# A column sum of 32768 x 2048 float32: from casting loads with TensorE sums to float32 loads with a running vector sum

## The chip, the core and the metric

The kernel runs on one core of one Trainium2 chip. The metric is the device time of one execution in microseconds. Before the change three runs gave a median of 629.03 us (628.92 to 629.57).

A core has five engines with queues of their own: TensorE (PE, matrix multiply, with PEld for its weight loads), VectorE (DVE), ScalarE (ACT), GpSimd (POOL) and SyncE (SP). DMA transfers are issued from the queue of an engine (here POOL or SP), and 16 DMA engines carry them out. SBUF is the memory on the core with 128 partitions, PSUM is where TensorE writes its sums, and DRAM holds the input and the output.

## The reference

```python
def setup_inputs():
    batch, seq, dim = 32, 1024, 2048
    return {"grad_output": np.random.randn(batch, seq, dim).astype(np.float32)}

def reference(grad_output):
    return np.sum(grad_output, axis=(0, 1)).astype(np.float32)
```

The input is 268.44 MB. Seen as 32768 rows of 2048 float32, it is 256 row blocks of 128 rows. The output is one row of 2048 float32. All the work is one pass over the input.

## The kernel before

The list `plan` (L60 to L85) cuts the 256 row blocks into loads, in this order: two float32 tiles of one row block each, issued from SP; 30 tiles of eight row blocks and one of two, then a taper of four and two, all issued from POOL; five tiles of one row block; and the last row block in four pieces of 512 columns, from the right column group to the left one. All loads from POOL have float16 tiles as their destination, so the DMA casts on the way. A tile of m row blocks gives each partition m neighbouring rows of DRAM, which is one contiguous piece of m x 8 KB.

One loop (L132) goes over the plan. It issues the load (L146). For a float16 tile of more than one row block it adds the tile's two halves on VectorE into `C` (L152, float16). Then it sums over the 128 partitions on TensorE (L161): a matmul with a column of ones as weights and 512 columns of `C` or of the tile as moving data adds one row of 512 sums to one of four PSUM accumulators, one for each group of 512 columns. An eight-row-block tile needs 16 such matmuls after the add. Behind the loop the four accumulators are copied to `res`, by ScalarE (L175) and VectorE (L177) in turn, and one DMA from SP writes the output (L178).

What sets the order: the Tile framework traces the instructions, puts them on the queues of their engines and adds the semaphore waits. Each queue is worked off in order. The pool "io" has three buffers for the large tiles, of 32 KB in each partition, so the load of tile i+3 on POOL waits until L152 has read tile i. The tail tiles have a pool of eight buffers of their own. The SP queue holds the two first loads and the output; POOL's queue holds the other 42 loads. The two float32 tiles are multiplied in float32 with `ones32`, the others in float16 with `ones16`.

```python
nc.vector.tensor_tensor(
    out=C[:], in0=T[:, :half], in1=T[:, half:], op=mybir.AluOpType.add
)
...
nc.tensor.matmul(
    accs[b][:, :],
    lhsT=w[:],
    rhs=red[:, j * MM_N : (j + 1) * MM_N],
```

Of the kernel before, what the change touches and what calls it, by code (L numbers as in the profile page):

```python
# [1 line left out]

# [4 lines left out]

P = 128
MM_N = 512  # L10

PRE_TILES = 2
PRE_M = 1
PRE_ENGS = ("sync", "sync")
BULK_M = 8
BULK_TAPER = (4, 2)
USE_DVE = True
TAIL_TILES = 5
COL_SPLIT_LAST = True
T_BUFS = 3  # L20
C_BUFS = 3
TAIL_BUFS = 8
BULK_ENGS = ("gpsimd",)
OUT_COPY_ENGS = ("scalar", "vector")


@with_exitstack
def kernel(
    ctx: ExitStack,
    tc: tile.TileContext,  # L30
    grad_output: bass.AP,
    out: bass.AP,
):
    nc = tc.nc
    fp32 = mybir.dt.float32
    fp16 = mybir.dt.float16

    D = out.shape[-1]
    flat = grad_output.rearrange("b s d -> (b s) d")
    R = flat.shape[0]  # L40
    assert R % P == 0 and D % MM_N == 0
    nbanks = D // MM_N
    n_row_blocks = R // P

    pre_tiles = min(PRE_TILES, n_row_blocks // PRE_M // 4)
    col_split = COL_SPLIT_LAST and nbanks > 1
    taper = [m for m in BULK_TAPER if m < BULK_M]
    n_small = TAIL_TILES + (1 if col_split else 0)
    while pre_tiles * PRE_M + sum(taper) + n_small > n_row_blocks:
        if TAIL_TILES and n_small > 1:  # L50
            n_small -= 1
        elif taper:
            taper = taper[1:]
        else:
            col_split = False
            n_small = min(n_small, 1)
            break
    n_tail = n_small - (1 if col_split else 0)

    plan: list = []  # L60
    row = 0
    for i in range(pre_tiles):
        plan.append((row, PRE_M, fp32, PRE_ENGS[i % len(PRE_ENGS)], 0, D))
        row += P * PRE_M
    tail_start = R - P * (n_small + sum(taper))
    bi = 0
    while row < tail_start:
        take = min(P * BULK_M, tail_start - row)
        plan.append((row, take // P, fp16, BULK_ENGS[bi % len(BULK_ENGS)], 0, D))
        bi += 1  # L70
        row += take
    for m in taper:
        plan.append((row, m, fp16, BULK_ENGS[bi % len(BULK_ENGS)], 0, D))
        bi += 1
        row += P * m
    for _ in range(n_tail):
        plan.append((row, 1, fp16, BULK_ENGS[bi % len(BULK_ENGS)], 0, D))
        bi += 1
        row += P
    if col_split:  # L80
        for b in range(nbanks - 1, -1, -1):
            plan.append((row, 1, fp16, BULK_ENGS[bi % len(BULK_ENGS)], b * MM_N, MM_N))
            bi += 1
        row += P
    assert row == R  # L85

    io_pool = ctx.enter_context(tc.tile_pool(name="io", bufs=T_BUFS))
    pre_pool = None
    if pre_tiles:
        pre_pool = ctx.enter_context(tc.tile_pool(name="pre", bufs=pre_tiles))  # L90
    c_pool = None
    if USE_DVE:
        c_pool = ctx.enter_context(tc.tile_pool(name="csum", bufs=C_BUFS))
    n_small_tiles = n_tail + (nbanks if col_split else 0)
    tail_pool = None
    if n_small_tiles:
        tail_pool = ctx.enter_context(
            tc.tile_pool(name="tail", bufs=min(n_small_tiles, TAIL_BUFS))
        )
    const_pool = ctx.enter_context(tc.tile_pool(name="const", bufs=1))  # L100
    psum_pool = ctx.enter_context(tc.tile_pool(name="psum", bufs=1, space=bass.MemoryType.PSUM))

    ones16 = const_pool.tile([P, 1], fp16)
    nc.vector.memset(ones16[:], 1.0)  # L104
    ones32 = None
    if pre_tiles:
        ones32 = const_pool.tile([P, 1], fp32)
        nc.vector.memset(ones32[:], 1.0)  # L108

    accs = [  # L110
        psum_pool.tile([1, MM_N], fp32, tag=f"psum{b}", name=f"psum{b}")
        for b in range(nbanks)
    ]
    res = const_pool.tile([1, D], fp32)

    def uses_dve(entry) -> bool:
        _, m, dt_, _, _, col_n = entry
        return USE_DVE and dt_ is fp16 and m > 1 and col_n == D

    def n_chunks(entry) -> int:  # L120
        _, m, dt_, _, _, col_n = entry
        n = (m * col_n) // MM_N
        return n // 2 if uses_dve(entry) else n

    total_mm = [0] * nbanks
    for e in plan:
        for j in range(n_chunks(e)):
            total_mm[((e[4] + j * MM_N) % D) // MM_N] += 1
    started = [False] * nbanks
    n_mm = [0] * nbanks  # L130

    for i, entry in enumerate(plan):  # L132
        row0, m, dt_, eng_name, col_lo, col_n = entry
        rows = flat[row0 : row0 + m * P]
        if col_n == D:
            src = rows.rearrange("(p m) d -> p (m d)", p=P)
        else:
            src = rows[:, col_lo : col_lo + col_n]

        if dt_ is fp16:  # L140
            big = m > 1 and col_n == D
            pool, tag = (io_pool, "T") if big else (tail_pool, "Ttail")
            T = pool.tile([P, m * col_n], fp16, tag=tag, name=f"t{i}")
        else:
            T = pre_pool.tile([P, m * col_n], fp32, tag="Tpre", name=f"t{i}")
        getattr(nc, eng_name).dma_start(out=T[:], in_=src)  # L146

        red = T
        if uses_dve(entry):
            half = (m * col_n) // 2  # L150
            C = c_pool.tile([P, half], fp16, tag="C", name=f"c{i}")
            nc.vector.tensor_tensor(  # L152
                out=C[:], in0=T[:, :half], in1=T[:, half:], op=mybir.AluOpType.add
            )
            red = C

        w = ones16 if dt_ is fp16 else ones32
        for j in range(n_chunks(entry)):
            b = ((col_lo + j * MM_N) % D) // MM_N
            n_mm[b] += 1  # L160
            nc.tensor.matmul(  # L161
                accs[b][:, :],
                lhsT=w[:],
                rhs=red[:, j * MM_N : (j + 1) * MM_N],
                start=(not started[b]),
                stop=(n_mm[b] == total_mm[b]),
            )
            started[b] = True

    bank_order = list(range(nbanks - 1, -1, -1)) if col_split else list(range(nbanks))  # L170
    for k, b in enumerate(bank_order):
        eng = OUT_COPY_ENGS[k % len(OUT_COPY_ENGS)]
        dst = res[:, b * MM_N : (b + 1) * MM_N]
        if eng == "scalar":
            nc.scalar.copy(out=dst, in_=accs[b][:, :])  # L175
        else:
            nc.vector.tensor_copy(out=dst, in_=accs[b][:, :])  # L177
    nc.sync.dma_start(out=out[None, :], in_=res[:])  # L178


# [1 line left out]
_INS = ['grad_output']  # L182
_OUTS = [((2048,), 'float32')]


# [23 lines left out]
```

## Time and profile before

| what | value |
|---|---|
| median of three runs | 629.03 us |
| span of the profiled execution, first to last instruction | 627.2 us |
| busy: PE, DVE, POOL | 195.1, 138.9, 22.6 us |
| L152, adds over 8192 float16 | 30 times, 4.425 us each |
| L161, matmuls on c, 512 columns, float16 | 496 records, 0.533 us on average |
| L146 from POOL, issue | 42 times, 0.538 us each |
| L146 from POOL, 8 row blocks: issue to landing | 53.1 us (median) |
| mean granted TensorE clock | 0.650 |
| DRAM read | 268.44 MB, 428 GB/s over the span |

The page of the profile shows one profiled execution. Its own time is the span of 627.2 us, which begins at the first and ends at the last instruction; a time of a run holds what lies around it as well, and the median of the runs is 1.8 us longer than this span. Rows of groups give the line, the engine, the operation, the tiles, the shapes and the mean length of one instruction; what stands behind the bar is the idle time before them and what ended it. In answers about stretches of time each row gives the busy time of each engine, the granted TensorE clock (1.00 is full), the busy share of the DMA engines and the GB/s that they wrote. A packet is one contiguous piece that one DMA engine moves. In those rows a packet counts where it starts, so a short stretch can show a share over 1 and the next one nearly 0.

### The profile page before, as it was taken

How to read it: one execution, taken by the hardware profiler on the slowest of the kernel's cores; microseconds unless marked ns; L12 is line 12 of the kernel's file. 1: busy time of each engine (PE TensorE's matmuls, PEld its weight loads, DVE VectorE, ACT ScalarE, POOL GpSimd, SP SyncE). 2: the span in 40 equal slices, each digit the busy share in tenths (PEclk: the TensorE clock that was granted, in tenths of full speed). 3: DMA queues.
4: the chain of work that ended last, by engine and by line, in shares of the span. 5: the costliest groups of instructions: out<-in, count | busy, mean ns of one | idle time of the engine just before them, and what ended most of it. 6: DMA issues, size and time to landing. Idle time of an engine off the chain costs nothing.

```text
span 627.2 us, 1267 instructions
## 1 busy us (share of the span) xinstructions
PE 195.1 (31%) x536; PEld 58.1 (9%) x536; DVE 138.9 (22%) x37; ACT 2.4 (0%) x3; POOL 22.6 (4%) x46
## 2 busy tenths in 40 slices
PE   3323320333203333123341134321333312343165
PEld 0001100011000111001110011100111000111011
DVE  0202222022220122211222202222022221122320
ACT  0000000000000000000000000000000000000000
POOL 1000000000000000000000000000000000000110
PEclk9677556775567665667655776656676567665677
DMA  9999999999999999999999999999999999999997
GB/s 242 226 234 201 234 201 234 202 232 203 232 203 232 203 232 203 232 204 230 205 230 205 230 205 230 205 230 206 228 207 228 207 224 211 224 211 221 206 206 139
DMA packets 6344, 135.36 MB, mean 216 GB/s; under 512 B 705, under 2 KB 1217, under 8 KB 1857
## 3 DMA queue, kind: packets, MB, share of 16 engines
q0 software_dynamic: 6048, 133.17, 98.9%
q1 hardware_dynamic: 290, 2.11, 0.9%
q8 instruction: 4, 0.07, 0.0%
q14 instruction: 2, 0.02, 0.0%
HBM read 268.44 MB, written 0.01 MB: 428 GB/s over the span
## 4 chain that ended last, share of the span: by engine, by line
another core or an unknown queue 66%; DVE 21%; DMA 11%; PE 1%; POOL 1%; issue 0%; DVEq 0%; POOLq 0%
DVE c L152 20%; DMA t<-in_grad_output_dram 11%; PE psum L161 1%; POOL t L146 1%; DVEq L152 0%; DVE res L177 0%; POOLq L193 0%
## 5 line engine op out<-in xcount | busy, mean ns | idle before, releaser
L161 PE MATMUL psum<-c,ones 128*1 128x512 f16 x496 | 175.9, 533 | 405.5 <-DVE c L152 405.5
L152 DVE TENSOR_TENSOR c<-t 128x8192 f16<-128x8192 f16 (+2 forms) x33 | 137.5, 4167 | 471.1 <-DMA t<-in_grad_output_dram 471.1
L161 PEld LDWEIGHTS <-ones 128*1 128x1 f16 x520 | 56.5, 109 | 537.5 <-issue 516.4
L146 POOL DMA_DIRECT2D t<-in_grad_output_dram x42 | 22.4, 538 | 590.4 <-DVE c L152 575.3
L161 PE MATMUL psum<-t,ones 128*1 128x512 f16 (+1 forms) x40 | 19.4, 639 | 23.5 <-DMA t<-in_grad_output_dram 23.5
L177 DVE COPY res<-psum 1x512 f32<-1x512 f32 x2 | 1.4, 679 | 13.9 <-PE psum L161 13.9
L161 PEld LDWEIGHTS psum<-t,ones 128*1 128x1 f32 x16 | 1.6, 106 | 27.5 <-DMA t<-in_grad_output_dram 14.1
L175 ACT COPY res<-psum 1x512 f32<-1x512 f32 x2 | 1.1, 575 | 621.1 <-PE psum L161 621.1
L175 ACT ACT_TABLE_LOAD x1 | 1.3, 1283 | 0.7 <-PEq L193 0.7
L104 DVE MEMSET ones<- 128x1 f16 x1 | 0.1, 59 | 0.8 <-PEq L193 0.8
L193 POOL MEMSET const-float32-0.0<- 128x1 f32 x1 | 0.1, 100 | 0.2 <-issue 0.2
L193 POOL MEMSET const-bfloat16-1.0<- 128x1 bf16 x1 | 0.1, 103 | 0.0
L193 POOL MEMSET const-float32-1.0<- 128x1 f32 x1 | 0.1, 100 | 0.0
L193 POOL MEMSET const-uint8-127<- 128x1 uint8 x1 | 0.1, 100 | 0.0
L108 DVE MEMSET ones<- 128x1 f32 x1 | 0.1, 59 | 0.0
## 6 DMA issues: line engine op xcount, KB each, us to landing
t<-in_grad_output_dram POOLq DMA_DIRECT2D x30, 4096.0 KB, 53.1
t<-in_grad_output_dram POOLq DMA_DIRECT2D x5, 512.0 KB, 20.4
t<-in_grad_output_dram SPq DMA_DIRECT2D x2, 1024.0 KB, 14.3
t<-in_grad_output_dram POOLq DMA_DIRECT2D x2, 1024.0 KB, 26.6
t<-in_grad_output_dram POOLq DMA_DIRECT2D x1, 2048.0 KB, 29.0
t<-in_grad_output_dram POOLq DMA_DIRECT2D x4, 128.0 KB, 16.1
out_dram<-res SPq DMA_DIRECT2D x1, 8.0 KB
```

The lines of the kernel that those rows point to most:

```text
L104: nc.vector.memset(ones16[:], 1.0)
L108: nc.vector.memset(ones32[:], 1.0)
L146: getattr(nc, eng_name).dma_start(out=T[:], in_=src)
L152: nc.vector.tensor_tensor(out=C[:], in0=T[:, :half], in1=T[:, half:], op=mybir.AluOpType.add)
L161: nc.tensor.matmul(accs[b][:, :], lhsT=w[:], rhs=red[:, j * MM_N : (j + 1) * MM_N], start=(not started[b]), stop=(n_mm[b] == total_mm[b]),)
L175: nc.scalar.copy(out=dst, in_=accs[b][:, :])
L177: nc.vector.tensor_copy(out=dst, in_=accs[b][:, :])
L193: nc = _bacc.Bacc("TRN2", target_bir_lowering=False, num_devices=1)
```

## The change

The new kernel reads every byte as float32 and issues every load from SP; POOL issues none. The first row block becomes the running sum `s`, by a load straight into it. Then come 30 tiles of eight row blocks and one of seven. Each is folded in place on VectorE: the upper half of the tile is added to the lower half, until one row block is left (8 to 4 to 2 to 1, or 7 to 4 to 2 to 1), and that one is added to `s`. An eight-row-block tile has adds over 8192, 4096, 2048 and 2048 elements of each partition, all float32. The ring has three slots, as before, of 64 KB in each partition.

TensorE works only at the end, in float32. The last eight row blocks share one more slot of the ring. Three and two of them are loaded whole. The last three are loaded in two parts: columns 0 to 1535 of all three ("left"), and then columns 1536 to 2047 ("right"). Each part has one PSUM accumulator. The function `into` adds one row block's part to it with four matmuls: the columns are cut into four equal pieces (384 wide for left, 128 for right), and piece i goes to partitions 32 i to 32 i + 31, with 32 columns of ones as weights, placed at column 32 i of the array. So the four pieces use four different column groups of TensorE. `s` goes through `into` after the first five of these row blocks. Left's accumulator is copied by ScalarE, right's by VectorE, and each has an output DMA of its own, which takes one partition of each column group.

In the order of the program SP's queue has: `s`, the 31 tiles, the three and two row blocks, left, the output of left, right, the output of right.

The core of the diff (the constants, the plan and the loop of before are removed):

```diff
-BULK_ENGS = ("gpsimd",)
-OUT_COPY_ENGS = ("scalar", "vector")
+NB = 4
+M = 8
+SLOTS = 3
+N_BULK = 30
+TAIL_V = (7,)
+TAIL_T = (3, 2)
+LAST = 3
+RIGHT = 512
...
+    parts = ((0, left), (left, RIGHT))
...
+    s = one.tile([P, D], f32, name="s")
+    ones = one.tile([P, 32], f32, name="ones")
+    nc.vector.memset(ones[:], 1.0)
+    acc = [psum.tile([P, 512], f32, name=f"acc{i}", tag=f"acc{i}") for i in range(2)]
...
+    def load(dst, row, m, lo=0, w=D):
+        src = flat[row : row + m * P].rearrange("(p m) d -> p m d", p=P)[:, :, lo : lo + w]
+        nc.sync.dma_start(out=dst.rearrange("p (m d) -> p m d", m=m), in_=src)
+
+    def into(part, t, off, last=False):
+        lo, w = parts[part]
+        g = w // NB
+        for i in range(NB):
+            nc.tensor.matmul(
+                acc[part][32 * i : 32 * i + 32, 0:g],
+                lhsT=ones[:],
+                rhs=t[:, off + i * g : off + (i + 1) * g],
+                start=not seen[part][i],
+                stop=last,
+                skip_group_check=True,
+                tile_position=(0, 32 * i),
+            )
+            seen[part][i] = True
+
+    load(s[:], 0, 1)
+    row = P
+    for m in (M,) * N_BULK + TAIL_V:
+        t = ring.tile([P, M * D], f32, name="t", tag="t")
+        load(t[:, : m * D], row, m)
+        row += m * P
+        while m > 1:
+            k = m - m // 2
+            nc.vector.tensor_tensor(
+                out=t[:, : (m - k) * D], in0=t[:, : (m - k) * D], in1=t[:, k * D : m * D], op=add
+            )
+            m = k
+        nc.vector.tensor_tensor(out=s[:], in0=s[:], in1=t[:, :D], op=add)
+
+    t = ring.tile([P, M * D], f32, name="t", tag="t")
+    off = 0
+    for m in TAIL_T:
+        load(t[:, off : off + m * D], row, m)
+        row += m * P
+        for j in range(m):
+            for p in range(2):
+                into(p, t, off + j * D + parts[p][0])
+        off += m * D
+    for p in range(2):
+        into(p, s, parts[p][0])
+    for p in range(2):
+        lo, w = parts[p]
+        load(t[:, off : off + LAST * w], row, LAST, lo, w)
+        for j in range(LAST):
+            into(p, t, off + j * w, j == LAST - 1)
+        off += LAST * w
+        if p:
+            nc.vector.tensor_copy(out=res[p][:], in_=acc[p][:, : w // NB])
         else:
-            nc.vector.tensor_copy(out=dst, in_=accs[b][:, :])
-    nc.sync.dma_start(out=out[None, :], in_=res[:])
+            nc.scalar.copy(out=res[p][:], in_=acc[p][:, : w // NB])
+        nc.sync.dma_start(
+            out=out[lo : lo + w].rearrange("(g d) -> g d", g=NB), in_=res[p][0:P:32, :]
+        )
```

More of the change, by code (lines that the diff above doesn't have):

```diff
@@ L9 @@
 P = 128
[L10 to L22, printed above, removed]
-BULK_ENGS = ("gpsimd",)
-OUT_COPY_ENGS = ("scalar", "vector")
+NB = 4
[6 more added lines that the diff above has]
+RIGHT = 512
 @with_exitstack
@@ L34 @@
     nc = tc.nc
-    fp32 = mybir.dt.float32
-    fp16 = mybir.dt.float16
+    f32 = mybir.dt.float32
+    add = mybir.AluOpType.add
     D = out.shape[-1]
     flat = grad_output.rearrange("b s d -> (b s) d")
[L40 to L53, printed above, removed]
-        else:
[L55 to L98, printed above, removed]
-        )
[L100 to L178, printed above, removed]
+    assert flat.shape[0] == P * (1 + M * N_BULK + sum(TAIL_V) + sum(TAIL_T) + LAST)
@@ new lines @@
+    left = D - RIGHT
+    parts = ((0, left), (left, RIGHT))
+    ring = ctx.enter_context(tc.tile_pool(name="ring", bufs=SLOTS))
+    one = ctx.enter_context(tc.tile_pool(name="one", bufs=1))
+    psum = ctx.enter_context(tc.tile_pool(name="psum", bufs=1, space=bass.MemoryType.PSUM))
+    s = one.tile([P, D], f32, name="s")
+    ones = one.tile([P, 32], f32, name="ones")
+    nc.vector.memset(ones[:], 1.0)
+    acc = [psum.tile([P, 512], f32, name=f"acc{i}", tag=f"acc{i}") for i in range(2)]
+    res = [one.tile([P, w // NB], f32, name=f"res{i}", tag=f"res{i}") for i, (_, w) in enumerate(parts)]
@@ new lines @@
+    seen = [[False] * NB, [False] * NB]
+    def load(dst, row, m, lo=0, w=D):
[15 more added lines that the diff above has]
+            seen[part][i] = True
```

## The prediction

> **What bounds the kernel now.** I read the page's busy row and slices first, then the queues, then the chain of waits in order of time, and last the stretches in which single loads can be timed.
>
> ```profile
> PE 195.1 (31%) x536; PEld 58.1 (9%) x536; DVE 138.9 (22%) x37; ACT 2.4 (0%) x3; POOL 22.6 (4%) x46
> ...
> DMA  9999999999999999999999999999999999999997
> ...
> q0 software_dynamic: 6048, 133.17, 98.9%
> q1 hardware_dynamic: 290, 2.11, 0.9%
> ...
> HBM read 268.44 MB, written 0.01 MB: 428 GB/s over the span
> ```
>
> No engine is busy for a third of the span, and the DMA engines never rest until the last slice. The bytes written are half of those read (float32 becomes float16 on the way), so the read side sets the pace.
>
> ```profile
> 144.37 4.42 DVE c L152
> 148.80 14.77 another core or an unknown queue
> ...
> 163.69 4.42 DVE c L152
> ```
>
> In the chain of waits the adds of L152 start 19.32 us apart (163.69 - 144.37), and 14.8 us of that is waiting for data. One period reads 1024 rows of 8 KB, 8.39 MB: 434 GB/s. One period is longer, 104.81 to 125.10 (20.29 us), a pause of 0.97 us.
>
> The next fence has three stretches (busy time by engine, granted clock, DMA share, GB/s written). In the first only line 146's two float32 loads on SyncE's queue move. The others are the end of the stream.
>
> ```profile
> 3.00:5.50 2.50, 0.00 (x0) 0.00 (x0) 0.00 (x0) 0.00 (x0) 0.00 (x0) 1.00 1.00 423
> ...
> 622.00:622.50 0.50, 0.50 (x2) 0.13 (x1) 0.00 (x0) 0.00 (x0) 0.00 (x0) 0.50 0.38 61
> 622.50:623.00 0.50, 0.50 (x2) 0.13 (x1) 0.00 (x0) 0.15 (x1) 0.00 (x0) 0.50 0.10 14
> ```
>
> Data stops at about 622.6. Behind it:
>
> ```profile
> 623.46 0.63 PE L161 MATMUL psum<-t,ones 128*1 128x512 f16 x1
> 624.13 0.68 DVE L177 COPY res<-psum 1x512 f32<-1x512 f32 x1 [0.17 <-PE psum L161]
> 624.90 0.32 SPq L178 DMA_DIRECT2D out_dram<-res  x1
> ```
>
> The last matmul ends at 624.1, the copy at 624.8, and the output needs 2.3 us from its issue to the end at 627.2. So the time is a stream at its limit and 4.6 us behind it. The three runs have a median of 629.03, 1.8 more than this span; I add 1.8 to every span below.
>
> **The stream (removed: casting loads by POOL; added: float32 loads by SP).** Bytes read stay the same; bytes written double. I fit one law to two rows. A DMA engine gets 8 packets of 64 KB in 19.32 us, 2.415 us each (casting). In 3.00:5.50 a float32 packet of 8 KB takes 16 x 8192 B / 423 GB/s = 0.310 us. With a fixed cost per packet both fit 27.24 GB/s per engine and 9 ns. A third row agrees: before's last casting tiles (8 KB read per packet) reach their matmuls at 613.11, 615.58, 618.02 and 620.52, 2.47 us each, and 8 x 0.310 is 2.48. So I take the float32 write to be free. By the law (8 packets per row block and engine, longer where rows of one partition lie together) after needs 2.48 (s) + 30 x 19.32 + 16.91 (7 rows) + 7.29 + 4.88 (3 and 2 rows) + 5.63 (left: 24 packets of 6 KB) + 2.02 (right: 24 of 2 KB) = 618.8; before needs 4.96 + 579.6 + 19.46 (2, 4, 2 rows) + 12.4 + 2.7 = 619.1. **Data ends 0.3 earlier, at 622.3**; 1.0 more is won if the pause at 105 to 125 doesn't come back. The other end: the 423 GB/s is a rate of float32 writes and not a cost per packet. Then 267.4 MB behind s take 632 us and not 616. I take the law, as it also explains the 8 KB packets that write float16.
>
> [...]
>
> Removed with POOL's loads: 42 issues of 0.54 us that nothing waited on. SP's issues (0.43 us each) lie under 19 us transfers. Three slots stay: a slot is free when the vector engine has finished its tile, and then one whole load is still queued.
>
> **The running sum.** Each 8-row tile gets adds over 8192, 4096, 2048 and 2048 elements (L152 had one, over 8192 float16). No float32 add is in the trace. Below: the float16 rows (8192 in 4.425, 4096 in 2.293, 2048 in 1.226 us, so 0.16 + 0.52 ns an element), 9.2 us a tile. Above: L177's copy, the only float32 row of this engine, 1.33 ns an element with its fixed cost, 21.7 us a tile. I take twice the float16 slope, since bytes double: 8.69 + 4.43 + 2.29 + 2.29 = 17.7, with 0.05 between adds 17.9. That hides under 19.32; past that it would set the pace.
>
> [...]
>
> For the end, count from the landing of the 7-row tile (0; data ends at 19.7). The 30th tile landed at -16.9, its adds end at +1.0, the 7-row tile needs 6.56 + 4.43 + 2.29 + 2.29 and gaps, 15.8: **s is complete at 16.9**, before left lands at 17.7. Nothing waits for it unless PE is early.
>
> **TensorE at the end.** The 496 matmuls on c and 24 on t in float16 go; they lay under the stream, so nothing is won but at the end. Eight row blocks and s stay, in float32:
>
> ```profile
> 25.86 0.13 PEld L161 LDWEIGHTS psum<-t,ones 128*1 128x1 f32 x1 [0.72 <-issue]
> 26.71 0.13 PEld L161 LDWEIGHTS psum<-t,ones 128*1 128x1 f32 x1 [0.72 <-issue]
> ...
> 28.59 0.08 PEld L161 LDWEIGHTS psum<-t,ones 128*1 128x1 f32 x1 [0.34 <-issue]
> 29.02 0.08 PEld L161 LDWEIGHTS psum<-t,ones 128*1 128x1 f32 x1 [0.34 <-issue]
> ```
>
> Eight float32 calls show 16 records, so each is two passes; passes over 512 columns come 0.85 us apart (clock 0.50) and 0.43 apart once the clock is granted, about 3 us into this burst. One row block is 2048 columns: 6.8 us slow, 3.4 fast, if the four groups run one after another. Whether groups run side by side no row shows. All four at once: 1.7 or 0.85 a block. Half of it, because the second pass of a group holds back the next group: 3.4 or 1.7.
> All at once: three blocks start at 7.3, two at 12.1, done by 13.8; PE idles 3.1 until s. The slices show the clock falling after 2.4 to 2.6 us of idling, so s starts slow, ends at 18.6 (17.8 if fast); left's three need 3 x 0.64 to 1.28, right's 3 x 0.21 to 0.43. PE ends 0.6 (fast) to 3.2 (slow) behind the data. Half: PE is behind from 7.3 on and ends at 24.3, 4.6 behind. One after another: about 40, 20 behind.
> I take 2.0 behind: side by side, partly slow, between the two clocks that the trace shows.
> Then the copy: 128 columns for 512, L177's 0.68 less 384 x 1.04 ns, 0.3; 0.1 to the issue; 2.3 for the output. Left's copy and output lie beside right's load.
>
> **Sum:** 622.3 + 2.0 + 0.3 + 0.1 + 2.3 = 627.0; less 0.5, half the pause, 626.5; with 1.8: **628.3 us**. Own range 626.4 (fast, no pause) to 630.0 (slow, with pause). The gain is small because the stream was at its limit already.
>
> **Rivals.**
> 1. *SP's order (slower).* In the code the store of left stands ahead of right's load, on one queue. If the queue keeps that order, right waits behind a store that waits for matmuls and a copy. For it: POOL kept its order in before, where seven loads, most with buffers of their own, started only at 593.61 behind one that waited for a slot. Against: right's load depends on nothing, so a planner may put it first. Price: left lands at 620.3, its matmuls end at 622.2 to 624.4, copy and store issue 1.0, right's load 4.3 (before's first load needed 4.97 for 1 MB, this has 0.79), matmuls 1, tail 2.7: 631 to 633.5, or 633 to 635.3 with 1.8. It decides as soon as that store is queued first.
> 2. *Groups overlap by half or not at all:* 622.3 + 4.6 + 2.7 + 1.8 = 631.4, or about 647.
> 3. *float32 writes bound the stream at 423:* 632.1 from 4.9 on, data ends at 637; about 642.
> 4. *The vector engine becomes the bound:* 21.7 us a tile, about 690. Twice the slope is the nearer row.
> 5. *Faster still:* a stream at 19.28 us a tile (no fixed cost seen), no pause, fast clock: about 625.5.
>
> **Chances.** Forecast 0.46, rival 1 0.20, rival 2 0.18 (0.12 half, 0.06 none), rival 3 0.08, rival 4 0.02, rival 5 0.06. About 0.2% (1.3 us) can be told from no change. Of the forecast 0.28 lies under 627.8 and 0.18 between that and 630.3; rival 5 is faster; half overlap without the pause is 630.4, at the border, so half of its 0.12 counts as within: faster 0.28 + 0.06 = 0.34, same 0.18 + 0.06 = 0.24, slower 0.20 + 0.12 + 0.08 + 0.02 = 0.42. The range is 625.8 to 635.5: it leaves out rival 3, 4, half of 5 and serial groups, 0.19. Both signs hold much; the forecast's own range is the one above.
>
> **What would show it.** Adds of 8192 float32 at 8.7 us and tiles 19.3 apart: stream and sum right. Tiles at 19.8: rival 3. Last load issued within microseconds of the others, or after left's copy: rival 1. Matmul records of the groups overlapping, and the gap from data end to last matmul: 2 us, 4.6 or 20. I am wrong if data ends later than 623.5 or if PE trails by over 3.2.

## The result, and the profile after

The changed kernel takes 631.27 us (median of five runs, 630.03 to 631.74) against 629.03 for the one before: a ratio of 1.0035, 95% interval 1.0022 to 1.0047. It is slower by about a third of a per cent, where 628.3 was forecast.

The profiled execution of the changed kernel took 631.74 us and has a span of 629.9 us, 1.8 less, as before. Its page first: the busy row, the DMA row of the 40 slices, SP's queue and the bytes.

```profile
PE 11.8 (2%) x144; PEld 5.1 (1%) x144; DVE 546.9 (87%) x126; ACT 1.8 (0%) x2; POOL 0.2 (0%) x4
...
DMA  9999999999999999999999999999999999999995
...
q1 hardware_dynamic: 5712, 268.45, 98.7%
...
HBM read 268.44 MB, written 0.01 MB: 426 GB/s over the span
```

The sum has moved from PE to DVE, and all loads to the hardware queue of SP, but the picture is the old one: the DMA engines never rest until the last slice. The float32 adds, by their groups (mean ns of one, then the idle time before them):

```profile
L79 DVE TENSOR_TENSOR t<-t 128x8192 f32<-128x8192 f32 x30 | 260.8, 8692 | 69.8 <-DMA t<-in_grad_output_dram 69.8
L79 DVE TENSOR_TENSOR t<-t 128x4096 f32<-128x4096 f32 x31 | 137.2, 4425 | 1.1
L83 DVE TENSOR_TENSOR s<-s,t 128x2048 f32<-128x2048 f32 x31 | 71.1, 2292 | 1.1
```

Those are 17.7 us of adds a tile, and the idle time in front of the first add is a wait for data, so DVE isn't the bound. The chain of waits shows the pace of the tiles:

```profile
335.49 8.70 DVE t L79
...
393.54 8.70 DVE t L79
```

These two adds are three tiles apart: 58.05 us, 19.35 a tile. One other tile takes 20.33, between the landings at 218.45 and 238.78, so the pause of 0.98 is back at another place. Next are the last instructions in order of time (what stands in brackets is the idle time before and its releaser); the weight loads are there because their distance is the distance of TensorE's passes.

```profile
618.14 2.29 DVE L83 TENSOR_TENSOR s<-s,t 128x2048 f32<-128x2048 f32 x1
620.48 1.07 PE L60 MATMUL acc<-s,ones 128*32 128x384 f32 x16 [2.33 <-DVE s L83]
...
621.87 4.33 PE L60 MATMUL acc<-t,ones 128*32 128x384 f32 x48 [0.32 <-DMA t<-in_grad_output_dram]
622.52 0.20 PEld L60 LDWEIGHTS acc<-t,ones 128*32 128x32 f32 x4 [0.44 <-issue]
623.16 0.20 PEld L60 LDWEIGHTS acc<-t,ones 128*32 128x32 f32 x4 [0.44 <-issue]
...
626.28 0.29 DVE L103 COPY res<-acc 128x128 f32<-128x128 f32 x1 [5.86 <-PE acc L60]
626.60 1.27 SPq L106 DMA_DIRECT2D out_dram<-res  x2
```

Six more rows are stretches of the end (granted clock, DMA share and GB/s stand last):

```profile
621.50:622.00 0.50, 0.18 (x8) 0.13 (x8) 0.00 (x0) 0.00 (x0) 0.00 (x0) 0.61 1.07 397
...
622.75:623.00 0.25, 0.25 (x4) 0.00 (x0) 0.00 (x0) 0.00 (x0) 0.00 (x0) 0.50 0.06 25
623.00:623.25 0.25, 0.25 (x8) 0.09 (x4) 0.00 (x0) 0.00 (x0) 0.00 (x0) 0.50 0.06 25
...
627.50:628.00 0.50, 0.00 (x0) 0.00 (x0) 0.00 (x0) 0.00 (x0) 0.00 (x0) 1.00 0.02 4
628.00:628.50 0.50, 0.00 (x0) 0.00 (x0) 0.00 (x0) 0.00 (x0) 0.00 (x0) 0.94 0.00 0
628.50:629.00 0.50, 0.00 (x0) 0.00 (x0) 0.00 (x0) 0.00 (x0) 0.00 (x0) 0.50 0.04 12
```

The last packets of data start between 623.0 and 623.25. The DMA share of 0.06 in front of that is one engine of 16: the others have no data left to start, and one trails them by some 0.9 us. At 621.6, between `s` and left, the granted clock falls to a half: the passes of left come 0.64 us apart, while those of `s` had come 0.32 apart. TensorE ends at 626.26. Both outputs are issued from 626.60 on, **right's ahead of left's**: right's 2 KB (4 GB/s over 0.5 us) move first and left's 6 KB (12 GB/s) one microsecond later, though left's sums had been in `res` since 626.11.

The two profiles side by side (us):

| step | before | after | difference |
|---|---|---|---|
| last data | 622.6 | 623.1 | +0.5 |
| from there to TensorE's end | 1.5 | 3.2 | +1.7 |
| from there to the issue of the output | 0.8 | 0.3 | -0.5 |
| from there to the end of the span | 2.3 | 3.3 | +1.0 |
| span | 627.2 | 629.9 | +2.7 |

So 2.2 of the 2.7 us came behind the last data, and 0.5 in the stream of 620 us in front of it. The runs of the changed kernel also lie in two groups, told apart by their mean granted clock: with the six runs of experiment 10, five of eleven at 0.999 or 1.000 (median 630.03 us) and six at 0.996 or 0.997 (median 631.60). The profiled one is of the second group. Below, versions are compared at equal clock wherever a version has both groups.

**The theory** that I went on to test: the end of the changed kernel costs two things that can be had back, the half clock (1.6 us) and right's and left's output behind one another (0.9). **The rivals:** one of them hides the other; the 0.03 us a tile come from SP's queue and not from float32; the column groups don't run side by side at all, and the tail is short for another reason.

### The profile page after: what moved, and what is told of

Same layout as the page of the kernel before. It is cut to its first block, busy times and chain, and to the rows that moved or that the text cites. A ratio compares the mean times of both kernels' runs of the same rounds, so it can differ in the third digit from the quotient of the medians.

```text
span 629.9 us, 531 instructions
## 1 busy us (share of the span) xinstructions
PE 11.8 (2%) x144; PEld 5.1 (1%) x144; DVE 546.9 (87%) x126; ACT 1.8 (0%) x2; POOL 0.2 (0%) x4
## 4 chain that ended last, share of the span: by engine, by line
DMA 70%; DVE 28%; PE 1%; SPq 0%; issue 0%
DMA t<-in_grad_output_dram 70%; DVE t L79 25%; DVE s L83 4%; PE acc L60 1%; SPq L54 0%; DVE res L103 0%
## 5 line engine op out<-in xcount | busy, mean ns | idle before, releaser
L79 DVE TENSOR_TENSOR t<-t 128x2048 f32<-128x2048 f32 (+3 forms) x93 | 475.5, 5113 | 72.0 <-DMA t<-in_grad_output_dram 69.8
L83 DVE TENSOR_TENSOR s<-s,t 128x2048 f32<-128x2048 f32 x31 | 71.1, 2292 | 1.1
L60 PE MATMUL acc<-t,ones 128*32 128x128 f32 (+1 forms) x128 | 10.7, 496 | 612.1 <-DVE t L79 611.4
L60 PEld LDWEIGHTS acc<-t,ones 128*32 128x32 f32 x128 | 4.7, 137 | 617.8 <-DVE t L79 611.4
```

The costliest lines, as they stand in the source:

```text
L60: nc.tensor.matmul(acc[part][32 * i : 32 * i + 32, 0:g], lhsT=ones[:], rhs=t[:, off + i * g : off + (i + 1) * g], start=not seen[part][i], ...
L79: nc.vector.tensor_tensor(out=t[:, : (m - k) * D], in0=t[:, : (m - k) * D], in1=t[:, k * D : m * D], op=add)
L83: nc.vector.tensor_tensor(out=s[:], in0=s[:], in1=t[:, :D], op=add)
```

## Experiments

**1. Left's output from ACT's queue.** The same work; only the queue of one store differs.

```diff
-        nc.sync.dma_start(
+        (nc.sync if p else nc.scalar).dma_start(
             out=out[lo : lo + w].rearrange("(g d) -> g d", g=NB), in_=res[p][0:P:32, :]
         )
```

> Left's output is issued from ScalarE's queue, behind left's copy, and no longer stands behind right's output on SyncE's queue. In the changed kernel left's copy ends at 626.11, yet both outputs are issued from 626.60 on, 0.6 us each, left's second, and its bytes start 0.9 us after right's. Theory (left's output is the last link, queued behind a store that it does not need): left's issue starts right after its copy, the stretch from right's copy to the end shrinks from 3.3 to 2.4 us, time down by 0.9 us. Rival (right's output, issued at the same moment as before, sets the end, and 3.3 us is what an output of four partitions needs): no change within 0.3 us.

Measured: 629.53 us, ratio 1.0016 (1.0007 to 1.0025). Eight of eleven runs held the clock (629.49), three didn't (630.94). At equal clock it is 0.5 us (630.03 - 629.49) and 0.7 us (631.60 - 630.94) faster than the changed kernel. (The kernel before had 628.81 beside this one and 629.03 and 628.88 beside those runs, so up to 0.2 of that need not be the edit's.) The end of its profile, in a run that held the clock:

```profile
621.51 2.80 PE L60 MATMUL acc<-t,ones 128*32 128x384 f32 x48 [0.32 <-DMA t<-in_grad_output_dram]
...
624.23 1.08 ACTq L106 DMA_DIRECT2D out_dram<-res  x1
...
624.70 0.66 SPq L106 DMA_DIRECT2D out_dram<-res  x1
```

The same matmuls take 2.80 us where they took 4.33. The issues of the two stores now overlap (624.23 to 625.31 and 624.70 to 625.36), and from the copy of right (624.38) to the end (627.4) it is 3.0 us where it was 3.6 (626.28 to 629.9). So left's store behind right's on one queue costs 0.5 to 0.7 and not 0.9: ACT needs 1.08 us for its issue, SP 0.66.

**2. TensorE kept busy while it waits for `s`.** Twelve matmuls into an accumulator that nobody reads, between the fifth row block and `s`.

```diff
+    keep(t, off - D, 3)
     for p in range(2):
         into(p, s, parts[p][0])
```

> Adds 12 matmuls (three row blocks' left part) into a spare accumulator that nothing reads, in TensorE's pause between the fifth row block and s (618.15 to 620.48 in the changed kernel). Theory (the clock fell to 0.50 in that pause, and left's and right's nine sets ran at half speed for the first 3 us): the clock stays at 1.00, passes of left come 0.32 us apart instead of 0.64, PE ends 1.8 us earlier behind left's landing (2.6 instead of 4.4 us), time down by 1.8 us. Rival 1 (the four groups in float32 are limited by their weight loads or their data, not by the clock): passes stay at 0.64, no change. Rival 2 (the pause is not what lowers the clock, it falls with the share of busy time): the clock still falls before left lands, gain under 0.5 us.

Measured: 630.65 us, ratio 1.0029 (1.0018 to 1.0041); all six runs held the clock (630.57 to 630.74). The end of its profile, and in a fence of its own one stretch:

```profile
621.68 2.14 PE L60 MATMUL acc<-t,ones 128*32 128x384 f32 x24 [0.32 <-DMA t<-in_grad_output_dram]
...
624.17 0.86 PE L60 MATMUL acc<-t,ones 128*32 128x128 f32 x24 [0.35 <-DMA t<-in_grad_output_dram]
```

```profile
623.50:623.75 0.25, 0.25 (x4) 0.00 (x0) 0.00 (x0) 0.00 (x0) 0.00 (x0) 1.00 0.04 16
```

With a gap of 0.41 us instead of 2.33 the clock never fell, and left took 2.14 us. But right's last packets started some 0.4 later than in the changed kernel, and right's matmuls waited for it. So against the low-clock runs only 0.95 of 1.57 came back, and against the high-clock ones it lost 0.6. Why the extra matmuls delay the last packets isn't known. The edit shortens the gap and also raises the share of time in which TensorE is busy, so it can't tell which of the two keeps the clock; the profiles can, further below.

**3. Both edits together**, experiments 1 and 2.

> Both edits: left's output from ScalarE's queue, and the 12 matmuls into a spare accumulator in TensorE's pause. Theory (two links in a row on the path that sets the end): the gains add, 1.8 + 0.9 = 2.7 us, to about 628.6 where the changed kernel has 631.3 and before 629.0. Rival (one hides the other): 1.8 or less.

Measured: 629.96 us, ratio 1.0020 (1.0011 to 1.0029), eleven runs, all with the clock held. That is 0.7 better than experiment 2 and 0.5 worse than the high-clock runs of experiment 1. The rival was right: the two gains don't add, since the late data takes the place of the late matmuls.

**4. Less work behind the last load.** Experiment 3 with two whole row blocks loaded after `s`, so that only one row block is cut into left and right.

```diff
-LAST = 3
+MORE = 2
+LAST = 1
```

> As both edits together, and only one row block (not three) is loaded last in left and right; two more go through TensorE before. Same bytes, same adds. Theory (the path behind the last byte is TensorE's work on what lands last): left's part of one row block is 0.64 us at full clock instead of 1.9, right's 0.2 instead of 0.6, so another 1.0 to 1.5 us goes, to about 627.3. Rival (the clock is lost because TensorE has more waits, or s arrives too late and holds the queue): within 0.5 us of both edits together.

Measured: 629.53 us, ratio 1.0013 (1.0004 to 1.0021). It gains 0.4 on experiment 3, where 1.3 was expected.

**5. The same without the extra matmuls** (experiment 1 with the shorter last part).

> Left's output from ScalarE's queue and only one row block last (two more go through TensorE before), without the 12 extra matmuls. With them the time was 629.53, their tail data landed up to 1 us later than without (last packets start at 623.5 to 623.75 against 622.75 to 623.0), and a packet of TensorE's code moved at 620.25 instead of 622.0. Theory (the extra matmuls bring TensorE's code packet of 1.1 us into the last loads): without them the code packet comes at the 49th to 52nd matmul, now in the second of the two more row blocks at about 621.5, and the time is 0 to 0.5 us less, about 629.2. Rival (extra matmuls only help by the clock): some runs show a low clock and the median is above 629.5.

Measured: 629.21 us, ratio 1.0013 (1.0005 to 1.0022). Eight runs held the clock (629.14), three didn't (630.63). At a held clock it is the fastest float32 version, 0.35 better than experiment 1 and 0.4 better than experiment 4 (the kernel before had 628.88 beside this one, and 628.81 beside those two). The extra matmuls cost time where the clock would have held (629.53 for 629.14), and save it where it wouldn't (629.53 for 630.63).

**6. Fewer and wider matmuls.** Experiment 5 with column groups of 512 columns: left takes groups 0 to 2 and right group 3, which makes 36 matmuls out of 72.

```diff
+    groups = ((0, 3), (3, 1))
...
-        g = w // NB
-        for i in range(NB):
+        first, n = groups[part]
+        for k in range(n):
+            i = first + k
```

> As the plain one-row-block-last kernel, but each column group takes 512 neighbouring columns: left is groups 0 to 2, right group 3, four matmuls a row block instead of eight, 36 in all. Theory (TensorE's code packet of 16 KB, asked for at about the 50th float32 matmul, takes one DMA engine out of the stream for 1.1 us just at its end): no code packet of that queue in the tail, the last load lands 0.5 to 1 us earlier; right's matmul is longer by 0.6 us and the copies by 0.3, so the time is 0.5 less to 0.4 more than the plain one. Rival (the packet delays nothing, the trailing engine is late from elsewhere): the last load lands when it did, and the time is 0.9 us more.

Measured: 629.56 us, ratio 1.0019 (1.0010 to 1.0027); 629.43 with the clock held (seven runs), 630.98 without (four). In this profile no code packet moves at the end (a packet of 16 KB with an engine's own instructions, 1.1 us on one DMA engine in experiment 5), and the data ends 0.1 us earlier than in experiment 5. But at a held clock it is 0.3 slower than experiment 5, as its last matmuls end later (24 of them in 3.29 us from 621.26 on, against 48 in 2.77 from 621.37) and a copy of 512 columns takes 0.70 us (experiment 12) where one of 128 takes 0.29, so the time doesn't tell what the packet costs.

**7. Loads from POOL.** Float32 as before, other queue.

```diff
-        nc.sync.dma_start(out=dst.rearrange("p (m d) -> p m d", m=m), in_=src)
+        (nc.gpsimd if row else nc.sync).dma_start(out=dst.rearrange("p (m d) -> p m d", m=m), in_=src)
```

> All loads but that of s are issued from GpSimd's queue instead of SyncE's, still float32 to float32. In the changed kernel tiles come 19.35 us apart, in before (casting loads from GpSimd) 19.325. Theory (the 0.025 us a tile, 0.8 us in all, comes with the queue that issues): 19.32 us a tile. Rival (it comes with the doubled bytes written): 19.35 us a tile. Either way the end of the stream moves by under 1 us, and the tail stays.

Measured: 630.03 us, ratio 1.0026 (1.0016 to 1.0036); 629.97 with the clock held (seven runs), 631.63 without (three): the same as the changed kernel. Its chain of waits, three tiles between the two rows:

```profile
44.35 8.70 DVE t L79
...
102.40 8.70 DVE t L79
```

58.05, again 19.35 a tile. The longer tile comes with the float32 loads and not with the queue.

**8. Packets of 8 KB.** The tiles' rows are dealt out so that a partition gets rows 128 apart, and a packet is one row.

```diff
-        load(t[:, : m * D], row, m)
+        nc.sync.dma_start(
+            out=t[:, : m * D].rearrange("p (m d) -> p m d", m=m),
+            in_=flat[row : row + m * P].rearrange("(m p) d -> p m d", p=P),
+        )
```

> Same bytes, same adds, another order of rows: a partition takes rows 128 apart in DRAM, so the 31 large tiles are read in packets of 8 KB instead of 64 KB (or 56 KB). The law of the prediction (27.24 GB/s for a DMA engine and 9 ns for a packet) says 8 x 8 x 0.310 = 19.84 us a tile, 0.49 more, 15 us in all: about 646. Rival (the 423 GB/s at the start of before were a start-up effect and packets cost nothing): 19.35 us a tile, no change.

Measured: 647.26 us, ratio 1.0292 (1.0271 to 1.0313), the median of two runs, one of each clock group (646.40 and 648.13). One stretch of the bulk, of this kernel first, then of the changed one:

```profile
25.00:218.00 193.00, 0.00 (x0) 0.00 (x0) 172.77 (x39) 0.00 (x0) 0.00 (x0) 1.00 1.01 422
```

```profile
25.00:218.00 193.00, 0.00 (x0) 0.00 (x0) 176.92 (x40) 0.00 (x0) 0.00 (x0) 1.00 1.00 435
```

A tile takes 19.88 us for 19.35. The law of the prediction (27.24 GB/s and 9 ns a packet) gives 64 x 0.310 = 19.84. So 423 GB/s at 3.00 to 5.50 was the price of short packets and not of float32.

**9. One column group.** Pieces of 512 columns, all on the first 32 columns of the array, one after another. The sums then stand in one partition, and the copies and stores follow that.

```diff
-        g = w // NB
-        for i in range(NB):
+        g = 512
+        for i in range(w // g):
...
-                tile_position=(0, 32 * i),
+                tile_position=(0, 0),
```

> TensorE's tail uses one column group: pieces of 512 columns one after another, all at the same place of the array, one partition of sums, copies of 1536 and 512 elements. Theory (the four groups of the changed kernel run side by side): a row block now takes four times as long, 6.8 us at the low clock and 3.4 at the high one; nine of them from the landing of the three row blocks at about 611.4 on end at about 643 to 646, 17 to 20 us later than the changed kernel's 626.3. Rival (the groups run one after another there too): TensorE ends where it does now, and only the copies are longer by about 2 us.

Measured: one run, 648.74 us; the kernel before had a median of 628.94 us beside it. Its matmuls:

```profile
611.26 19.09 PE L59 MATMUL acc<-t,ones 128*32 128x512 f32 x40 [611.26 <-DVE t L78]
630.19 3.60 PE L59 MATMUL acc<-s,ones 128*32 128x512 f32 x8
```

`s` takes 3.60 us where four groups take 1.07. The groups do run side by side; one after another they would end 18 us later (644.1 for 626.3).

**10. The changed kernel again.**

> The changed kernel itself again, beside the others on one chip. Its five runs so far fall in two groups: 630.03 with a mean granted clock of 0.999, and 631.03 to 631.74 with 0.996 to 0.997; the same two groups stand in the runs with left's output on ScalarE's queue (629.2 to 629.6 and 630.7 to 631.0) and with the loads from GpSimd's queue (629.8 to 630.2 and 631.4 to 631.7). Theory (the clock of TensorE, up or down when left lands, makes the two groups): two groups 1.4 to 1.6 us apart, told apart by the clock alone. Rival (the spread is the stream's): times between the groups, and no order by the clock.

Measured: 630.13 us (629.97 to 631.76), ratio 1.0027 (1.0016 to 1.0039): four runs with the clock held (630.06), two without (631.61 and 631.76). The profile of one of the two shows the same end as above: a gap of 2.34 us, then passes 0.64 apart.

**11. The column groups alone, in the kernel before.** Its loads, casts, adds and pieces are as they were; the four accumulators lie on four column groups, with 32 columns of ones.

```diff
-                accs[b][:, :],
+                accs[b][32 * b : 32 * b + 32, :],
...
+                tile_position=(0, 32 * b),
```

> The kernel before with one part of the change alone: its four accumulators are put in four column groups (32 columns of ones as weights), and the output leaves from four partitions. Loads, casts and adds stay. Theory (four groups side by side are the gain of the change, the float32 stream and two outputs its loss): the last eight matmuls of before, which come 0.43 us apart at the low clock and end at 624.1, 1.5 us behind the last data, take about 0.9 us instead of 3.6; the time falls by 0.5 to 1.0 us under before, to about 628. Rival (weight loads of 32 columns, or the low clock with less work, eat it up): no change from before within 0.2 us.

Measured: 629.04 us, ratio 1.0003 (0.9994 to 1.0012): no change. Sixteen matmuls on one add's result now take 1.90 us (at 168.22) where they took 5.12, but TensorE had waited 17.42 us in front of them, so they were hidden, and at the end each of the four last pieces waits for its data:

```profile
620.58 3.19 PE L161 MATMUL psum<-t,ones 128*32 128x512 f16 x8 [1.88 <-DMA t<-in_grad_output_dram]
...
623.81 0.68 DVE L178 COPY res<-psum 1x512 f32<-1x512 f32 x1 [0.66 <-PE psum L161]
```

The last copy starts at 623.81 (before: 624.13), and the output with four rows takes 0.64 us to issue where it took 0.32.

**12. The casting stream with the new end:** column groups, the last row block cut into 1536 and 512 columns, left's output on ACT.

> Before's loads, casts and adds with the parts of the change that did not cost: four column groups of 512 columns, the last row block in two pieces (1536 and 512 columns, not four of 512), left's copy and output on ScalarE's queue, right's on VectorE and SyncE. In before with the groups alone the four last pieces were ready 0.65 us apart, from 621.8 to 623.8, and the last copy ended at 624.5. Theory (the end of before is set by four small loads that land one after another): two pieces land earlier, right is copied by about 624.1, and the time is 0.3 to 0.8 us under before, about 628.3. Rival (the last load lands when the trailing DMA engine is done, however it is cut): no change from before within 0.2 us.

Measured: 628.61 us against 628.84, ratio 0.9997 (0.9988 to 1.0006). That can't be told from the kernel before. No version beat the kernel before.

## Why the prediction was wrong, step by step

The span was put at 626.5 us and is 629.9. The 3.4 us between them are three terms of the sum; the sign turned on them. The measured 631.27 us lies above the forecast's own range (626.4 to 630.0), whose slow end had the low clock and the pause but neither of the other two losses. It lies inside the wide range of 625.8 to 635.5, but the upper part of that stood for rivals 1 and 2, which didn't happen; that it holds is luck.

- **The tail: "I take 2.0 behind: side by side, partly slow, between the two clocks that the trace shows."** This is the step that failed first. The clock at the end of this kernel has two values, and a middle is what no profile shows. The profiled run had 3.2 (+1.2); the profile of experiment 1, with the clock held, has 1.4 (624.31, data to 622.9). The two ends, 0.6 and 3.2, were in the working, and so was the cause: the slices' "2.4 to 2.6 us of idling" and a pause worked out as 3.1. (The slow end holds with `s` at full clock, as it came. With `s` slow too, as the working has it, its own terms end at 23.7, 4.0 behind.) The pause was 2.33, and the mean clock is the lower one in six of eleven runs. Experiments 2 to 4 show that the pause costs the clock: filled with matmuls up to the last 0.4 us, the clock held in all 28 runs.
- **The output: "2.3 for the output. Left's copy and output lie beside right's load."** They didn't: left's copy ended at 626.11, after the last data, and its store stood behind that of right, which waits for the last copy. The output took 3.3 (+0.9 with the copy and the issue). I weighed what SP's order does to a load (rival 1) and didn't ask what it does to the other store. Experiment 1 puts 0.5 to 0.7 on it. The rest is the issue of a store with four rows: 0.66 for one (experiment 1), 0.32 before.
- **The stream: "I take the float32 write to be free", and "half the pause".** The law is right for packets (experiment 8: 19.88, worked out 19.84). But a float32 tile takes 19.350 and a casting one 19.324 (medians), which is 0.8 us over 30 tiles, and the pause came back whole, another 0.5. Data ended at 623.1 and not 621.8 (+1.3). Experiment 7 excludes the queue; why float32 loads cost 0.03 us a tile stays open. The two bounds that I set, 623.5 for the data and 3.2 for the tail, were both kept: neither sign showed that three smaller losses add up.
- **The adds** were right to the last digit that the rows have: 8.69, 4.43, 2.29, 2.29 (measured 8.692, 4.425, 2.292, 2.292), so **rival 4** was out. `s` was complete 1.4 us before left landed; 0.8 was worked out (the loads behind the 7-row tile add up to 19.8 by its terms, not 19.7).
- **Side by side** was right: `s` takes 1.07 us against 3.60 in experiment 9, of which half overlap would leave 1.8. **Rival 2** was out.
- **Rival 1** as I put it didn't happen: right's load was issued ahead of left's store. What did was its small brother: stores in an order that the program doesn't have.
- **Rival 3** (642) was excluded by the bulk, which ran at 435 GB/s (a tile: 8.39 MB in 19.35 us, 434 GB/s) with every byte written as float32, and **rival 5** by tiles of 19.35 us and the pause.

**What decides the clock.** The profiles show it falling after gaps of 2.33 and 2.34 us (the changed kernel, experiment 10) and 1.89 (experiment 8), and holding after 1.64 to 1.93 (experiments 1, 5, 6 and 7) and 0.39 to 0.41 (experiments 2 to 4). So the length of the gap doesn't decide. Of the 43 runs of experiments 1, 5, 6 and 7, 13 have the lower mean clock. The traces have a better measure. In the kernel before 3.41 us or a multiple of it, up to 17.07, lie between two recorded changes of the clock; in the changed kernel it falls at 621.61, returns at 625.02 and falls at 628.44. The next rows are steps of 3.41 us, counted from such changes, that hold the gap. The first two end with a fall (the changed kernel, then experiment 8), and in the third the clock held (experiment 1). TensorE's busy time stands behind the length of the step.

```profile
618.20:621.61 3.41, 1.07 (x16) 0.42 (x16) 2.23 (x1) 0.00 (x0) 0.00 (x0) 1.00 1.01 401
```

```profile
635.10:638.51 3.41, 1.48 (x24) 0.63 (x28) 1.12 (x1) 0.00 (x0) 0.00 (x0) 1.00 1.00 385
```

```profile
616.82:620.23 3.41, 1.68 (x36) 0.85 (x32) 3.21 (x2) 0.00 (x0) 0.00 (x0) 1.00 1.00 411
```

With 1.07 to 1.48 us of matmuls in the step the clock fell, and with 1.68 to 1.77 (experiments 1, 5, 6 and 7) it held. In the kernel before, all 32 recorded falls follow steps with at most 41% of matmuls, and it held behind steps with 42% and more. The 1.48 us of experiment 8 are 43%, so the line is known to a few per cent only (the ends of matmuls are modelled). Where the steps lie differs from run to run. In the changed kernel's profile the five row blocks ended at 618.15, just ahead of the step; in experiment 1 they ran until 618.39, inside it. That would make the two groups a matter of where the steps happen to lie, and the clock of a single run a matter of luck. It is worked out from the profiles; no experiment moved the steps, and the runs without a profile show only their mean clock.

**What is shown and what is argued.** Shown: the side-by-side groups (1.07 us for 3.60), that filling the gap with matmuls keeps the clock (28 runs of 28), that left's store behind right's costs 0.5 to 0.7, that the longer tile isn't the queue's (19.35 us from SP and from POOL). Argued only, from profiles set against each other: that the busy share of a step decides the clock, and that the 0.8 us of the longer tiles reaches the end in full. Open: why float32 tiles are longer, why extra matmuls delay the last load, and what the pause is.

## What to carry to other kernels

Where a stream at its limit sets the time, a change of engine behind it can gain only in the last microseconds (here 4.6 of 627.2), so count these instruction by instruction, the stores' order on their queue included. A cost with two values (here a clock that held or fell, 630.03 or 631.60 us) isn't to be averaged: take one, give the other its own chance, and ask what decides between them: by the profiles here, the share of busy time and not the length of one gap. Two gains at the end need not add (629.96 us with both edits here, where their sum was put at 628.6), since the next one late may already be there: here, data.

## What the runs showed of the hardware that was not expected

- **A code packet lies where one tile is late.** One tile of the kernel before is late by 0.97 us and one of the changed kernel by 0.98; in experiments 7 and 8 the same three tiles that hold the changed kernel's are late by 0.73 and 0.76 together. In the stretch of the late tile one DMA engine moves a packet of an engine's code. The rows, of the kernel before at 113.50 to 114.00 and of the changed one at 237.00 to 237.50 (queue, packets, MB, share of 16 engines in the stretch):

```profile
q8 instruction: 1, 0.02, 12.2%
```

```profile
q14 instruction: 1, 0.01, 4.1%
```

  That is 0.98 us (12.2% of 0.5 us x 16) of one engine in a tile that is 0.97 late, and 0.33 in one that is 0.98 late. Other code packets of the kernel before made no tile late (at 577.5, for one: 0.89 us of one engine, in a tile of 19.36). That they are the cause wasn't tried. One engine of 16 that falls behind and never catches up would fit both the late tile and the engine that trails at the end; this wasn't tried either.
- **The clock column starts at 1.00, whatever the clock.** In the changed kernel it shows 1.00 at 611 to 615, but the first weight loads (611.38, 612.03, 612.67) come 0.64 us apart, the slow distance; only from 615.1 on it is 0.32. In experiment 11 it shows 1.00 all along, with passes 0.43 apart, the slow distance for 512 columns at before's 0.50. The distance of the passes is the better witness, and the mean clock tells runs apart only where a fall was recorded.
- **The issue of a store** took 0.32 us for one row on SP (the kernel before, experiment 12), 0.56 to 0.66 for four rows there, and on ACT 1.07 to 1.08 for four rows of 384 columns and 1.28 for three rows of 512.
